# Log-sum-exp over 1024 columns: the row four from last loaded in five strided parts, 9 rows for each of eight DMA engines and 7 for each of the others

## The chip, the cores and the metric

One core of one Trainium2 chip. The metric is the device time in microseconds (us) of one execution; smaller is better. The span of a profiled execution is some 1.4 us shorter than its time.

## The reference

```python
# x: float32 (32, 512, 1024), axis = -1
x_max = np.max(x, axis=axis, keepdims=True)
return (x_max.squeeze(axis) + np.log(np.sum(np.exp(x - x_max), axis=axis))).astype(np.float32)
```

The inputs are standard normal numbers, so the kernel leaves the maximum out and computes the logarithm of the sum of exponentials.

## The kernel before

Each of the 128 partitions takes 128 rows of x that follow one another in HBM, 4 KB each. They arrive in 17 loads of falling size (4, 15, 16, 16, 16, 14, 13, 9, 7, 5, 4, 3, 2, 1, 1, 1, 1 rows a partition), all issued by SyncE into a ring of 51 rows. ScalarE (ACT) takes exponentials; VectorE (DVE) or ACT's own accumulator sums them. "Row" below is one such row of every partition: a load of 128 x 4 KB. The last four loads are one row each and all ACT's.

```python
CHUNKS = [  # rows, rows that DVE sums, parts, by halves
    # ... cut: eight loads
    (7, 7, 1, True), (5, 4, 1, True), (4, 3, 1, True), (3, 3, 1, False), (2, 2, 1, True),
    (1, 0, 1, False), (1, 0, 1, False), (1, 0, 1, False), (1, 0, 1, False),
]
# ...
    x_v = x_flat.rearrange("(p t) d -> p t d", p=P)
# ...
    def load(i):
        (s, row), r = place[i], CHUNKS[i][0]
        # ... cut: waits until the ring's rows are free
        nc.sync.dma_start(out=ring[:, s : s + r], in_=x_v[:, row : row + r]).then_inc(
            landed[i], 16
        )
# ... in the loop over loads:
        if i == len(CHUNKS) - 1:
            take_logs(logged, late_row, sums[:, logged:late_row], *done_before[-LATE])
        nc.scalar.wait_ge(landed[i], 16)
        # ... cut: exponentials for the rows that DVE sums
        for j in range(n_dve, r):
            nc.scalar.activation(out=ring[:, s + j], in_=ring[:, s + j], func=Exp,
                                 accum_out=total(row + j)).then_inc(act_done, 1)
# ... after the loop: the logarithm of the last four sums, and the store of 64 KB
```

The softmax here doesn't subtract the row's maximum and nothing guards it: scores larger than these inputs give would overflow.

## Time and profile before

| | |
|---|---|
| time, median of the first 3 runs | 162.7 us (162.52 to 162.91) |
| time, median of 6 runs, with those beside the changed kernel | 162.77 us (162.45 to 163.13) |
| span of the profiled execution | 161.5 us |
| landing of the load of three rows (12th) | 150.93 us |
| landing of the load of two rows (13th) | 153.42 us |
| landings of the last four rows | 154.70, 155.99, 157.27, 158.50 us |
| start of the last exponential | 158.56 us |

A landing is the last of the sixteen completions that the trace records for a load. The packets of the trace can be linked, each starting 3 to 9 ns before the one ahead ends, into sixteen strings, which I take for the sixteen DMA engines. Over the last six loads every string has eight packets of a load and then one of 4 bytes, its completion, load after load in the order of issue.

### The profile page before, as it was taken

Reading aid. Unit: us, or ns where it says so; the run is one execution under the profiler, and the core shown is the slowest. Engines: PE = TensorE matmul, PEld = TensorE weight load, DVE = VectorE, ACT = ScalarE, POOL = GpSimd, SP = SyncE. Lnnn points to the kernel's source line nnn. Section 1 sums busy time; section 2 is a strip of 40 time slices with the busy share of each in tenths; the row PEclk is TensorE's granted clock in tenths of the full one; section 3 lists DMA queues with packets and bytes.
Section 4 is the critical chain, followed back from the end, with each engine's and each line's share of the span. In section 5 each row is a group of like instructions: output and inputs, shape, how many; then the busy total and the mean of one; then the engine's idle time right before and its main releaser. Section 6 shows DMA issues by size and latency. Waiting matters only on the chain.

```text
span 161.5 us, 126 instructions
## 1 busy us (share of the span) xinstructions
DVE 121.0 (75%) x46; ACT 115.1 (71%) x40; POOL 0.2 (0%) x4
## 2 busy tenths in 40 slices
DVE  0028000004999999999999599999999999999892
ACT  3170006995079960999519993999199999999995
POOL 0000000000000000000000000000000000000000
DMA  7999899989799799699799999999899999999991
GB/s 268 495 487 457 350 411 520 406 373 520 308 471 520 325 455 520 276 503 520 325 422 455 455 455 438 422 422 422 366 429 438 444 433 406 441 414 423 405 407 36
DMA packets 2592, 67.18 MB, mean 416 GB/s; under 512 B 288, under 2 KB 416, under 8 KB 928
## 3 DMA queue, kind: packets, MB, share of 16 engines
q1 hardware_dynamic: 2592, 67.18, 97.3%
HBM read 67.11 MB, written 0.07 MB: 416 GB/s over the span
## 4 chain that ended last, share of the span: by engine, by line
DMA 49%; DVE 29%; ACT 20%; issue 0%
DMA ring<-in_x_dram 49%; DVE sums L157 29%; ACT ring L137 17%; ACT ring L164 3%; ACT res L108 0%
## 5 line engine op out<-in xcount | busy, mean ns | idle before, releaser
L157 DVE TENSOR_REDUCE sums<-ring 128x8 f32<-128x8192 f32 (+5 forms) x14 | 111.2, 7995 | 37.4 <-ACT ring L137 37.2
L137 ACT ACTIVATE ring<-ring 128x8192 f32<-128x8192 f32 (+6 forms) x18 | 104.4, 5836 | 44.0 <-DMA ring<-in_x_dram 43.9
L144 DVE CUSTOM_DVE_ANT_0 ring<-ring 128x512 f32<-128x512 f32 x16 | 9.9, 688 | 0.0
L164 ACT ACTIVATE ring<-ring 128x1024 f32<-128x1024 f32 x9 | 9.3, 1042 | 0.0
L122 ACT ACT_TABLE_LOAD x1 | 1.3, 1283 | 0.8 <-PEq L209 0.8
L164 ACT ACTIVATION_READ_ACCUMULATOR ring<-ring 128x1 f32 x9 | 1.6, 173 | 0.0
L144 DVE DVE_READ_ACCUMULATOR2_ANT sums<- 128x1 f32 x16 | 1.4, 85 | 0.0
L108 ACT ACTIVATE res<-sums 128x81 f32<-128x81 f32 (+1 forms) x2 | 0.5, 248 | 0.0
L108 ACT ACTIVATE res<-late 128x4 f32<-128x4 f32 x1 | 0.2, 173 | 0.0
L209 POOL MEMSET const-bfloat16-1.0<- 128x1 bf16 x1 | 0.1, 102 | 0.0
L209 POOL MEMSET const-uint8-127<- 128x1 uint8 x1 | 0.1, 102 | 0.0
L209 POOL MEMSET const-float32-0.0<- 128x1 f32 x1 | 0.1, 99 | 0.2 <-issue 0.2
L209 POOL MEMSET const-float32-1.0<- 128x1 f32 x1 | 0.1, 99 | 0.0
## 6 DMA issues: line engine op xcount, KB each, us to landing
ring<-in_x_dram SPq DMA_DIRECT2D x1, 7680.0 KB, 24.8
ring<-in_x_dram SPq DMA_DIRECT2D x1, 7168.0 KB, 29.0
ring<-in_x_dram SPq DMA_DIRECT2D x1, 6656.0 KB, 36.2
ring<-in_x_dram SPq DMA_DIRECT2D x1, 4608.0 KB, 20.3
ring<-in_x_dram SPq DMA_DIRECT2D x2, 2048.0 KB, 16.1
ring<-in_x_dram SPq DMA_DIRECT2D x1, 3584.0 KB, 28.4
ring<-in_x_dram SPq DMA_DIRECT2D x1, 2560.0 KB, 27.4
ring<-in_x_dram SPq DMA_DIRECT2D x4, 512.0 KB, 27.1
```

The source lines that it names most:

```text
L108: nc.scalar.activation(out=res[:, lo:hi], in_=src, func=Ln).then_inc(act_done, 1)
L122: nc.scalar.preload_act_table_set("natural_log_exp_and_others")
L137: nc.scalar.activation(out=ring[:, s + lo : s + hi], in_=ring[:, s + lo : s + hi], func=Exp).then_inc(act_done, 1)
L144: nc.vector.tensor_tensor_reduce(out=ring[:, s + j, : D // 2], in0=ring[:, s + j, : D // 2], in1=ring[:, s + j, D // 2 :], scale=1.0, scal ...
L157: nc.vector.reduce_sum(out=sums[:, row + lo : row + hi], in_=ring[:, s + lo : s + hi], axis=AX).then_inc(dve_done, 1)
L164: nc.scalar.activation(out=ring[:, s + j], in_=ring[:, s + j], func=Exp, accum_out=total(row + j),).then_inc(act_done, 1)
L209: nc = _bacc.Bacc("TRN2", target_bir_lowering=False, num_devices=1)
```

## The change

The sixteen completions of the last load lie 0.66 us apart (157.84 to 158.50). The intent is to give the early eight one row more and the late eight one less, once, near the end, so that the last landing comes sooner.

```diff
+UNEVEN = (13,)
+PARTS = ((0, 128, 2), (1, 128, 4), (3, 128, 8), (7, 64, 8), (71, 128, 8))
...
-        nc.sync.dma_start(out=ring[:, s : s + r], in_=x_v[:, row : row + r]).then_inc(
-            landed[i], 16
-        )
+        dst, src = ring[:, s : s + r], x_v[:, row : row + r]
+        if i not in UNEVEN:
+            nc.sync.dma_start(out=dst, in_=src).then_inc(landed[i], 16)
+            return
+        for first, last, step in PARTS:
+            nc.sync.dma_start(
+                out=dst[first:last:step], in_=src[first:last:step]
+            ).then_inc(landed[i], 16)
...
-        nc.scalar.wait_ge(landed[i], 16)
+        nc.scalar.wait_ge(landed[i], 16 * (len(PARTS) if i in UNEVEN else 1))
```

The parts have 64, 32, 16, 8 and 8 partitions: meant are 4, 2 and 1 rows for each engine, then 1 and 1 more for eight of them. "The first eight" below are the engines that take a load of eight partitions.

## The prediction

> **What bounds the kernel now.** The page of the run before gives two rows that matter at once, and I read them first:
>
> ```profile
> DVE 121.0 (75%) x46; ACT 115.1 (71%) x40; POOL 0.2 (0%) x4
> DMA  7999899989799799699799999999899999999991
> q1 hardware_dynamic: 2592, 67.18, 97.3%
> ```
>
> No compute engine is full, and the DMA row is at nine tenths or more in most slices: packets fill 97.3% of the span of 16 engines. The kernel is a stream of 67.11 MB from HBM, and compute follows it. The one question is what the end looks like: which wait ends last once the stream runs out. The changed load is one of four last loads of one row a partition (128 x 4 KB, 512 KB each), so only the last 10 us are concerned. The chain of work that ended last, from there on (start us, length us, what):
>
> ```profile
> 122.49 24.74 DMA ring<-in_x_dram
> 147.23 0.02 issue
> 147.26 2.76 ACT ring L137
> 150.02 1.04 ACT ring L164 x2
> 151.06 4.46 ACT ring L137 x2
> 155.52 3.01 ACT ring L164 x6
> 158.53 0.02 ACT res L108
> 158.55 0.01 issue
> 158.56 1.11 ACT ring L164 x2
> 159.67 0.02 issue
> 159.69 0.17 ACT res L108
> ```
>
> The last DMA on this chain landed at 147.23 us: that is the load of four rows, three loads ahead of the changed one. From there ScalarE (ACT) goes from one exponential to the next to 159.67 without a link to a DMA. So the last four loads are not named as what ended anything. How near they are to it is read from the time of issue and the time to landing of each of the four, taken alone: 129.0 + 25.7 = 154.7 us, 129.3 + 26.7 = 156.0, 129.8 + 27.5 = 157.3 and 130.3 + 28.2 = 158.5. Beside them stand the four exponentials that read them, in the timeline of ACT (start, length, engine, line):
>
> ```profile
> 155.42 1.04 ACT L164 ACTIVATE ring<-ring 128x1024 f32<-128x1024 f32 x1
> 156.42 1.05 ACT L164 ACTIVATE ring<-ring 128x1024 f32<-128x1024 f32 x1
> 157.42 1.05 ACT L164 ACTIVATE ring<-ring 128x1024 f32<-128x1024 f32 x1
> 158.42 0.24 ACT L108 ACTIVATE res<-sums 128x43 f32<-128x43 f32 x1
> 158.56 1.04 ACT L164 ACTIVATE ring<-ring 128x1024 f32<-128x1024 f32 x1
> ```
>
> Start less landing: 0.72, 0.42, 0.12 and 0.06 us. DMA delivers a row every 1.28 us, ACT uses one every 1.00 us, so ACT's lead melts by 0.28 a row and is gone at the last. An exponential that did wait for its load started 0.03 us after the landing (147.23 to 147.26), so the last one has a true slack of about 0.03 us. ACT's own order gives nearly the same start: the logarithm ahead of it began at 158.42 and the earlier logarithm of 81 columns held ACT for 0.16 us (128.31 to 128.47); this one of 43 columns, 38 fewer at 0.86 ns each (8192 columns took 7.01 us), should hold it for some 0.13, which gives 158.55 against 158.56 seen. ACT and the stream meet here within 0.03 us.
>
> [...] So parts of 64, 32 and 16 partitions give each engine 4, 2 and 1 rows, and the two parts of 8 give one more each to the first eight: 9 and 7. The trace agrees for the even load: 16 increments for each load, spread from 157.84 to 158.50 us for the last one, 0.66 us between first and last engine. It records no engine numbers, so which eight are early is not to be read.
>
> [...] Here a partition's rows lie 512 KB apart, and the steps make it 1, 2 and 4 MB. The trace shows only the 512 KB case, at 416 GB/s.
>
> **The change part by part.** No instruction of ACT, VectorE or GpSimd moves; SyncE issues five transfers in place of one.
>
> Issue: an issue of a row takes 0.33 to 0.46 us and one follows another every 0.37 to 0.48 (128.95, 129.33, 129.80, 130.28). Four more cost 4 x 0.48 = 1.9 us, so the last load is issued at 132.2 instead of 130.3. The data before it still land up to 154 us: the queue is over 20 us deep, and nothing of this reaches the path.
>
> Packets: a 4 KB packet takes 0.159 us in the best case (up to 0.172), each starting 3 ns before the one ahead ends, so 0.156 us an engine; a completion packet of 4 bytes adds about 6 ns. An engine of the first eight gets one packet and four completions more: +0.156 + 0.024 = +0.18 us. One of the others gets one packet fewer and two completions more: -0.156 + 0.012 = -0.14 us. All later loads go through the same queues in order, so these shifts stay up to the last landing.
>
> If the first eight are the early half (157.84 to 158.13), they end at 158.31 and the late half (158.14 to 158.50) at 158.36: the last landing comes 0.14 us earlier. That is the intent. But ACT gives only what its own order leaves: the last exponential can start 0.01 to 0.03 us earlier, not 0.14. Behind it come 1.11 us of exponential and its accumulator read, 0.17 of logarithm and 1.6 us of the store, all unchanged. So in the best case the change is worth 0.02 us, and about 0.1 us in executions where the stream runs a little later against ACT.
>
> In the other direction there is no cushion: a delay D of the slowest engine comes out at the end as D - 0.03 us.
>
> **The rivals.** First, the early half isn't the first eight. The completion times show a smooth spread (neighbours 0.01 to 0.12 us apart) and no gap between two halves, and the packet starts of the first load do not predict who finishes it first. Then some late engine gets +0.18 and the last landing moves to 158.68 at most: the end +0.15 us. What speaks for the intended half is only that somebody chose which half gets more.
>
> Second, the strided parts run slower than the plain row: [...]rows 4 MB apart. If that halved the rate, the packets of the row would take twice as long, 9 x 0.156 = 1.4 us more at worst; if it concerns only the three single-packet parts, 3 x 0.16 = 0.5. [...] In the profile before nothing tests it. It would make 163.1 to 164.1 us.
>
> Third, the four exponentials start to wait earlier (row three from last has 0.42 us of slack, the next 0.12). A delay above those shows as waits, but each only forwards the same D; they don't add up.
>
> **Range and chances.** Best case (-0.02 to -0.1) 0.35; a late engine loaded more (+0.15) 0.25; some slowing of the strided parts (+0.2 to +0.6) 0.3; a strong one (up to +1.4) 0.1. The middle of these is about +0.1 us on 162.7. The three runs before lie 0.39 us apart (162.52 to 162.91), which is more than the effect. I say 162.8 us, and 162.4 to 163.5. For 2% it would take 3.3 us in either direction: more than twice the worst rival, and more than the whole tail of ACT after the last landing for a gain. Faster 0.005, same 0.98, slower 0.015.
>
> **What would show it right or wrong.** In the trace after: increments of the changed load as 64 instead of 16 within the same stretch; the last landing near 158.36 (early half chosen), near 158.68 (not), or later than 158.8 (strided parts slow). The chain should still show ACT from about 147.26 on if the first holds, and a DMA as the last link before the last exponential if not. Packets of 4 KB over 0.2 us long during the changed load would show the [...]pitch rival. The prediction fails by over 0.7 us if the strided parts keep engines waiting between descriptors.

The forecast's sum came to -0.14 us at the last landing and -0.01 to -0.03 at the end in the best case, and, over all the cases, to a middle of about +0.1 us on 162.7, so 162.8. The trace after bears out the 9 and 7, and the strings of the trace before the order of the loads.

## More of the kernel before

What the stream moved near the end is in the stretches of time of the profile (stretch, length, then busy us and count of each engine, clock, DMA's busy share, GB/s):

```profile
151.00:152.00 1.00, 1.00 (x3) 1.00 (x2) 0.00 (x0) 1.00 1.04 434
153.30:154.30 1.00, 0.55 (x1) 1.00 (x2) 0.00 (x0) 1.00 1.05 418
```

The stream is full (share about 1) and moves 418 GB/s while the fourth row from last is on its way.

## The result, and the profile after

| | before | after |
|---|---|---|
| time, median of 6 runs | 162.77 us (162.45 to 163.13) | 162.69 us (162.48 to 162.92) |
| span of the profiled execution | 161.5 us | 161.2 us |
| landing of the load of three rows | 150.93 us | 150.53 us |
| landing of the load of two rows | 153.42 us | 153.03 us |
| last landing | 158.50 us | 158.22 us |

The ratio is 0.9996, with a 95% interval of 0.9979 to 1.0013. (A ratio is the mean time of one kernel's fast runs over that of the other's of the same rounds, so not quite the ratio of the medians.) The time is the same: what the change does is smaller than this interval, which is some 0.28 us to either side. The traces resolve much less than that, if one does not compare clock times. Loads that the change does not touch already land 0.4 us earlier in the trace after (150.53 for 150.93). So I count from the landing of the load of three rows, which is well ahead of the changed one, to the last landing: **7.57 us before, 7.69 after**. The last landing came 0.12 us later, not earlier.

First the page of the profile after, its count of DMA packets and the queue's share:

```profile
DMA packets 2640, 67.18 MB, mean 417 GB/s; under 512 B 336, under 2 KB 464, under 8 KB 976
q1 hardware_dynamic: 2640, 67.18, 97.4%
```

The 48 packets more than the 2592 of before are all tiny: completions, 64 in place of 16. Linked as before, each packet starting 3 to 15 ns before the one ahead ends, the trace gives eight strings with 4, 2, 1, 1 and 1 packets of the changed row and eight with 4, 2 and 1, a completion after each group: 9 and 7 as meant. (Where two packets end together the link is a choice; this one uses every packet from the load of three rows to the last.) Then the same two stretches of the trace after:

```profile
151.00:152.00 1.00, 1.00 (x5) 1.00 (x1) 0.00 (x0) 1.00 0.97 401
153.30:154.30 1.00, 0.94 (x1) 1.00 (x2) 0.00 (x0) 1.00 1.04 311
```

While the parts are moved, the engines are as busy as before (1.04) and move a quarter less: 311 GB/s for 418. The packets themselves say it: none of the 512 packets of 4 KB took over 0.19 us before (longest 0.172); after, 69 did, the longest 0.255, all of them begun between 153.28 and 154.38 us. The first 64 of 4 KB, as many as the part of step 2 has, were still at 0.16 to 0.17.

Last the tail of ACT in the timeline after:

```profile
157.03 1.05 ACT L175 ACTIVATE ring<-ring 128x1024 f32<-128x1024 f32 x1
158.03 0.24 ACT L119 ACTIVATE res<-sums 128x43 f32<-128x43 f32 x1
158.25 1.06 ACT L175 ACTIVATE ring<-ring 128x1024 f32<-128x1024 f32 x1
```

The last exponential starts 0.22 us after the logarithm, against 0.145 before (158.416 to 158.561), and 0.024 us after the last landing at 158.22. Now it waits for the load: 0.08 us. The chain of work that ended last does not name that wait:

```profile
155.12 3.02 ACT ring L175 x6
158.14 0.13 ACT res L119
158.27 0.00 ACT ring L175
158.27 0.94 issue
159.21 0.16 ACT ring L175
```

There is no DMA in it: ACT's instructions overlap (the exponential starts at 158.25 us, the logarithm ends at 158.27), so the gap that the load left probably is too small to appear as idle time; the exponential's own time is put down as "issue". A wait of under 0.1 us must be read from starts and landings.

### The profile page after: what moved, and what is told of

It reads as the page before. It is cut to its first block, busy times and chain, and to the rows that moved or that the text cites. A ratio compares the mean times of both kernels' runs of the same rounds, so it can differ in the third digit from the quotient of the medians.

```text
span 161.2 us, 130 instructions
## 1 busy us (share of the span) xinstructions
DVE 121.0 (75%) x46; ACT 115.2 (71%) x40; POOL 0.2 (0%) x4
## 4 chain that ended last, share of the span: by engine, by line
DMA 49%; DVE 29%; ACT 20%; issue 1%
DMA ring<-in_x_dram 49%; DVE sums L168 29%; ACT ring L148 17%; ACT ring L175 3%; ACT res L119 0%
```

## The experiments

All on one measure, from one trace each: from the landing of the load of three rows to the last landing ("stream"), and from the same landing to the end of the span ("tail"). D is the stream less 7.57. For the two-row load, which some expectations count from, the parts' first packets can already be in its way: in the trace after the first starts at 151.87 us, and that load lands at 153.03. Rows an engine, where an expectation names them, are as meant: counted are those of before (8) and after (9 and 7) alone.

| kernel | stream | D | tail | log to last exponential | 4 KB packets over 0.19 us | longest |
|---|---|---|---|---|---|---|
| before | 7.57 | | 10.54 | 0.145 | 0 | 0.172 |
| after | 7.69 | 0.12 | 10.64 | 0.223 | 69 | 0.255 |
| probe_before | 7.59 | 0.02 | 10.57 | 0.145 | 0 | 0.188 |
| probe_after | 7.70 | 0.13 | 10.67 | 0.230 | 62 | 0.291 |
| even_four | 7.82 | 0.25 | 10.77 | 0.221 | 71 | 0.338 |
| even_four_packed | 7.74 | 0.17 | 10.69 | 0.224 | 49 | 0.247 |
| blocks_9_7 | 8.46 | 0.89 | 11.42 | 0.229 | 172 | 0.364 |
| halves | 9.08 | 1.51 | 12.02 | 0.208 | 170 | 0.339 |
| step2_two | 7.56 | -0.01 | 10.53 | 0.145 | 0 | 0.172 |
| step8_eight | 9.22 | 1.65 | 12.18 | 0.204 | 199 | 0.472 |
| step8_packed | 8.89 | 1.32 | 11.84 | 0.224 | 175 | 0.375 |
| deal_step2 | 8.08 | 0.51 | 11.03 | 0.228 | 118 | 0.316 |
| all_four_9_7 | 9.25 | 1.68 | 12.20 | 0.444 | 211 | 0.282 |
| early_last | 6.96 | -0.61 | 10.54 | 0.145 | 0 | 0.172 |

Each line is one trace, and the traces come from several chips. Two pairs of near-equal kernels (before and probe_before, after and probe_after) lie 0.01 to 0.03 us apart, and in all 14 traces the load of three rows, which no change touches, lands 8.57 to 8.60 us after the load of five rows. So differences of 0.1 are safe to read.

A second measure from the same traces does not depend on which engine is last: the time of all 512 packets of 4 KB, shared over 16 engines, less that of before. It is 0.26 us in after and in even_four alike, 0.14 in even_four_packed, 1.20 in halves, 1.55 in step8_eight, 1.29 in step8_packed and 0.00 in step2_two. The slow packets are not all packets of the parts: halves had 170 where the changed row has 128. So rows beside it were slowed too; which packets those were was not worked out.

My theory at this point: the first eight engines are the early ones, the deal gains what was worked out, and the strided parts lose more. The rivals: the wrong half, and the uneven deal itself.

### Which engines are early: probe_before

```diff
+PROBES = (13, 15)
...
+        if i in PROBES:   # ahead of the fourth and the second row from last
+            n = PROBES.index(i)
+            nc.sync.dma_start(out=scratch[:, n], in_=x_v[0:8, n, 0:128]).then_inc(probed[n], 16)
```

> The kernel before, with two tiny loads (8 partitions, 512 bytes each) ahead of the fourth and the second load from last, each with a semaphore of its own[...]. Beside them stand the sixteen completions of the load just ahead. Theory 'intended half' (the first eight are the early ones): the eight probe completions match the eight earliest of the sixteen, within about 0.05 us. Theory 'no order': they are mixed among the sixteen, with at least two among the four latest. Last landing counted from the landing of the load ahead of the fourth from last: 5.1 us (5.08 in the profile before), within 0.1; end as before.

Which engines a load of eight partitions takes was given by a rule; what is measured is that it has eight completions.

The completions in the trace, in order of time (us):

```
two-row load   152.87 .91 .93 .96 .97 .97 153.01 .04 | 153.15 .16 .21 .26 .28 .33 .46 .53
probe          153.09 .11 .12 .15 .16 .17 .20 .22    (eight, and one of the sequencer at issue)
4th from last  154.17 .21 .24 .27 .28 .30 .31 .36    | 154.41 .43 .48 .52 .53 .61 .73 .81
```

The probe's eight come 0.18 to 0.22 us behind the eight earliest (not within the 0.05 that I expected), in nearly the same spacing; the late eight are spread over 0.38 us and the probe's over 0.14. The next load is a second witness: the eight earliest need 1.30 to 1.33 us for it, the others 1.25 to 1.28, so the earliest are those that carried the probe. The first eight are the early half here; their mean is 0.34 us ahead. "No order" falls.

### The parts without the deal: even_four

```diff
-PARTS = ((0, 128, 2), (1, 128, 4), (3, 128, 8), (7, 64, 8), (71, 128, 8))
+PARTS = ((0, 128, 2), (1, 128, 4), (3, 128, 8), (7, 128, 8))
```

> The same row in four strided parts (steps 2, 4, 8, 8) of 64, 32, 16, 16 partitions, so each engine moves 8 rows. Theory 'strided parts are slow': packets of 0.20 to 0.25 us appear again, last landing 5.25 to 5.45 us after the load ahead (before 5.08, changed kernel 5.19), spread between first and last engine still about 0.66. Rival 'the uneven deal alone is what moves the landing': packets stay at 0.16 to 0.17 us and the last landing is 5.08 to 5.15.

The last landing came 5.33 us after the two-row load; D is 0.25. The same stretch:

```profile
153.30:154.30 1.00, 1.00 (x1) 1.00 (x1) 0.00 (x0) 1.00 1.02 320
```

Slow packets without any unevenness: the parts cost 0.25 us, and the deal is not their cause. Against it, the changed kernel's 0.12 means that the deal takes 0.13 off, near the 0.14 that it was to bring. The packets took 0.26 us an engine longer in both, so the parts cost the same with and without the deal. Counted from the mean completion of the three-row load in place of its last, the deal takes 0.08 off: some 0.1 is what two traces support.

### Does the deal reach the engines: probe_after

The same two probes in the changed kernel.

> The changed kernel with the two tiny probe loads (8 partitions[...]), one ahead of the fourth row from last and one ahead of the second from last. In the kernel before with the probes the first eight were the eight earliest at both places. If the deal of 9 and 7 does what it intends: the first eight are still the earliest at the first probe, and at the second they are mixed with the others or late (0.18 + 0.14 = 0.32 us closer than before). If the deal does not reach the engines[...]: still the eight earliest at the second probe.

At the first probe the eight are again the earliest (153.08 to 153.26, 0.18 to 0.22 behind the eight earliest of the load ahead). At the second, less the same 0.2 us, they stand at 155.93 to 156.11, in the middle of the sixteen (155.82 to 156.27). The spread of the last row is 0.42 us where it was 0.58 with probes before (without probes 0.56 for 0.67). The deal does what it intends.

### Another way to 9 and 7: blocks_9_7

```diff
-PARTS = ((0, 128, 2), (1, 128, 4), (3, 128, 8), (7, 64, 8), (71, 128, 8))
+PARTS = ((0, 112, 1), (112, 120, 1), (120, 128, 1))
```

> 9 and 7 rows again, but in three unbroken blocks of 112, 8 and 8 partitions instead of strides. Theory 'strided parts are slow' with the intended half early: packets stay near 0.16 us and the last landing is about 4.95 us after the load ahead. With the wrong half: 5.2 to 5.3 with packets at 0.16. Rival 'any part of few partitions is slow, strided or not': packets of over 0.2 us, landing over 5.15.

5.72 us after the two-row load, D = 0.89. My theory in its form "strides are slow" falls: without a stride it is worse. Something else of the parts is slow. The slow packets began at 152.19 us, 0.40 us after the first packet of the row, when, by an estimate from 0.156 us a packet, no engine can have been past its third packet. The large part comes first, with seven rows an engine if dealt evenly. So the part of 112 partitions is among the slow ones, not only the two of 8.

### The whole at four times the size: all_four_9_7

```diff
-UNEVEN = (13,)
+UNEVEN = (13, 14, 15, 16)
```

> All four last rows dealt 9 and 7 in five strided parts. Theory 'strided parts cost some 0.29 us an engine and row' (mean shift of the sixteen completions in the changed kernel): 4 x 0.29 = 1.2, and the first eight 4 x 0.18 - 0.33 = 0.4 later than the late half was: last landing some 1.5 us later, time 164.1 to 164.5. Rival 'the parts cost nothing but the deal': +0.4 us, 163.1; wrong half: +0.7, 163.4.

164.17 us (163.93 to 164.46, 5 runs) against 162.37 for before on the same chip: ratio 1.0113 (1.0098 to 1.0128). D = 1.68, and the time rose by 1.80, the same within the noise. Here clock times show the cost most plainly (deal_step2, below, shows a smaller one), and it goes with the parts being slow; the deal alone would have made +0.4 or +0.7.

### HBM or the SBUF side: even_four_packed, halves

even_four_packed has the parts of even_four and this:

```diff
-                out=dst[first:last:step], in_=src[first:last:step]
+                out=dst[first:last:step], in_=x_flat[first * P : first * P + len(range(first, last, step))]
```

> Four strided parts, 8 rows an engine, as in the run with the even deal, but each part reads rows that lie one after another in HBM (a pitch of 4 KB in place of 1, 2 and 4 MB); the SBUF side is the same. The result is wrong on purpose. Theory 'the pitch in HBM makes the parts slow': packets back to 0.16 to 0.17 us and the last landing 5.05 to 5.15 us after the load ahead. Theory 'the SBUF side[...]': packets of over 0.2 us again, last landing 5.25 to 5.45.

"SBUF side" means here only what is left when the addresses in HBM are not the cause.

5.24 us, just under the range of the SBUF side and outside that of the pitch; 49 slow packets for 71. By itself undecided. (The record calls the runs with wrong results, this one, step8_packed and early_last, correct: its check does not notice such errors.)

```diff
-PARTS = ((0, 128, 2), (1, 128, 4), (3, 128, 8), (7, 64, 8), (71, 128, 8))
+PARTS = ((0, 64, 1), (64, 128, 1))
```

> The row in two unbroken halves, partitions 0 to 63 and 64 to 127: no stride, 8 rows an engine, 512 KB pitch in HBM as in the kernel before. Theory 'pitch in HBM' and theory 'strides': no slow packets, last landing 5.05 to 5.15 us after the load ahead. Theory 'SBUF side': [...]packets of up to 0.31 us and the last landing up to 8 x 0.156 = 1.25 us later, about 6.0 to 6.3; at least 5.5.

6.07 us after the two-row load, D = 1.51. The stretch again:

```profile
153.30:154.30 1.00, 0.86 (x1) 0.75 (x2) 0.00 (x0) 1.00 1.10 250
```

No stride and the pitch of before, and the rate fell from 418 to 250 GB/s with busy engines. The HBM pitch cannot be the cause here. Nor is it the number of parts: step2_two, below, has two parts as well and loses nothing.

### Which part: step2_two, step8_eight, step8_packed

```diff
-PARTS = ((0, 128, 2), (1, 128, 4), (3, 128, 8), (7, 64, 8), (71, 128, 8))
+PARTS = ((0, 128, 2), (1, 128, 2))                   # step2_two
+PARTS = tuple((k, 128, 8) for k in range(8))         # step8_eight and step8_packed
```

step8_packed also reads rows that lie one after another, as even_four_packed does.

> The row in two parts of step 2 (even and odd partitions, 64 each, 4 rows an engine each): 8 rows an engine. In the changed kernel the packets were still 0.16 us while most engines were in the part of step 2, and over 0.2 only after it. Theory 'the parts of step 8, one row an engine, are the slow ones': few or no packets over 0.19 us, last landing 7.57 to 7.65 us after the landing of the load of three rows (7.57 and 7.60 before, 7.82 with the four even parts). Rival 'any part of fewer than 128 partitions is slow, as the two halves were': 7.8 or later.

> The row in eight parts of step 8 (16 partitions, one row an engine each): 8 rows an engine. Theory 'the parts of step 8 are the slow ones': packets of 0.2 to 0.3 us over the whole row, last landing at 8.1 or later (8 packets, each at least 0.06 slower, +0.5 on 7.6). Rival 'only the change from one dealing to another is slow': 7.85 or less.

> The same eight parts of step 8, each read from rows that lie one after another in HBM (wrong on purpose), so the 4 MB pitch is gone and the SBUF side stays. Theory 'HBM pitch': last landing 7.6 to 7.75. Theory 'SBUF side': within 0.15 of the run with the pitch. Both together: in between.

One line of each, in this order: the first two parts cost nothing, the eight cut the rate to about a half.

```profile
153.30:154.30 1.00, 0.88 (x1) 1.00 (x2) 0.00 (x0) 1.00 1.01 406
```

```profile
153.30:154.30 1.00, 0.69 (x1) 0.39 (x2) 0.00 (x0) 1.00 1.01 225
```

```profile
153.30:154.30 1.00, 1.00 (x1) 0.71 (x1) 0.00 (x0) 1.00 1.09 250
```

D is -0.01, 1.65 and 1.32. Parts of 64 partitions with step 2 are free; those of 16 with step 8 are slow. Packing the rows takes off 0.33 of 1.65, which is what was expected for "both together", and 0.08 of 0.25 in the four parts (of the packets' time 0.26 of 1.55 and 0.12 of 0.26). So the pitch may have a share, from one look each: a small one in the eight parts, a third to a half in the four. With the source packed, most of the loss in the eight parts remains, which leaves the SBUF side or the way the rows are dealt.

### A deal of step 2 alone: deal_step2

```diff
-PARTS = ((0, 128, 2), (1, 128, 4), (3, 128, 8), (7, 64, 8), (71, 128, 8))
+PARTS = ((0, 128, 2), (1, 97, 2), (97, 113, 2), (113, 128, 2))
```

> 9 and 7 rows again, with step 2 alone: parts of 64, 48, 8 and 8 partitions (4, 3, 1 and 1 rows). Theory 'step 8 is the slow part, the deal itself is right': last landing 7.43 to 7.55, earlier than before; the last exponential starts 0.145 us after the logarithm (ACT bound) and the time is still that of before within noise. Rival 'the short parts are slow whatever their step': 7.65 or later and the last exponential waits for it.

D = 0.51, 163.05 us (162.88 to 163.44, 4 runs) against 162.54: ratio 1.0025 (1.0009 to 1.0042). Theory "step 8 alone is slow" falls too: a small step does not save this deal. The run does not tell the part of 48 partitions from the two of 8.

### What an earlier landing is worth: early_last

```diff
+        w = D // 2 if i == len(CHUNKS) - 1 else D
-        nc.sync.dma_start(out=ring[:, s : s + r], in_=x_v[:, row : row + r]).then_inc(
+        nc.sync.dma_start(out=ring[:, s : s + r, :w], in_=x_v[:, row : row + r, :w]).then_inc(
...
+                scale=1e-3 if i == len(CHUNKS) - 1 else 1.0,
```

> The kernel before with the last load cut to 512 of 1024 columns, so that it lands some 0.6 us earlier; the last exponential still covers 1024 columns (half of them stale, scaled by 0.001 so that nothing overflows; the result is wrong on purpose). Theory 'ACT's own order leaves only 0.01 to 0.03 us': the last exponential starts 0.12 to 0.14 us after the start of the logarithm ahead of it, not 0.145, and the time is that of before within noise, 0 to 0.1 us faster. Rival 'the last landing sets the end': 0.5 to 0.6 us faster.

The last landing came at 157.34 us, 0.61 earlier on the measure of the table. The tail of ACT:

```profile
157.86 0.24 ACT L109 ACTIVATE res<-sums 128x43 f32<-128x43 f32 x1
158.00 1.04 ACT L165 ACTIVATE ring<-ring 128x1024 f32<-128x1024 f32 x1
```

The last exponential starts 0.145 us after the logarithm (157.859 to 158.004), to the nanosecond what it did before and not the 0.12 to 0.14 that I expected, and the tail is 10.54, as before. The time is 162.34 against 162.56 with a ratio of 0.9997 (0.9980 to 1.0015). So in this trace nothing is to be had from an earlier last landing; the times alone would not resolve a gain of 0.1 us.

## Why the prediction was right, and where it was not

The time, 162.69 us for 162.8 predicted, is inside 162.4 to 163.5 and the same as before. That alone says little, since the noise is wider than the effect. By its steps:

- **The meeting of ACT and the stream within 0.03 us: right, and the delay passes through as D - 0.03.** The table tests it over a wide range: 10.54 + D - 0.03 gives 10.63 for after (measured 10.64), 10.76 for even_four (10.77), 11.40 for blocks_9_7 (11.42), 12.02 for halves (12.02) and 12.16 for step8_eight (12.18).
- **The best case of 0.01 to 0.03 us: too large.** I worked out that the logarithm of 43 columns would hold ACT for 0.13 us. early_last shows 0.145 with the data there for 0.6 us. ACT's order was the whole bound and the gain of an earlier landing was zero in that trace. The gain of about 0.1 us that I gave to executions with a later stream was not tested.
- **The deal of -0.14 us: right within what can be read**, 0.13 (0.08 on the other count) by even_four against after. That the first eight are the early half was left at better than even; the probe shows it, in these executions.
- **The strided parts: the rival happened, at a smaller size than its figures.** I gave 0.5 us if the three parts of single rows were slow; the row cost 0.25. Of the reasons given with it one, rows 4 MB apart, is no cause in halves (512 KB, D = 1.51) and a small one in step8_eight (0.33 of 1.65), but in even_four, the nearest to the change, packing took off a third of D (0.08 of 0.25). The argument against a strong slowing did not hold for parts that are slow throughout: in step8_eight the packets took 1.55 us an engine longer, where a doubling of 8 packets of 0.156 would be 1.25.
- **The sum failed in its mixture, not in its middle.** I weighed a best case against slow parts as alternatives. Both came at once: -0.13 from the deal and +0.25 from the parts make +0.12, of which 0.03 fell into ACT's slack, so some +0.09 at the end. The middle of my weights was +0.1; that the two agree is luck, since no entry of my list had both.
- **Issue: off, without effect.** I took 4 x 0.48 = 1.9 us. A strided part took 0.57 to 0.66 us to issue for 0.33 of the plain row, and the next row's issue came 3.22 us after the first part, not 0.37: 2.85 us more. The data in front still filled the queue until 153 us.
- **The signs to look for: partly badly chosen.** I gave clock times (158.36, 158.68, 158.8) for the last landing. 158.22 would have read as the gain, when the whole stream was 0.4 us ahead in that execution. Only the distance from an untouched load tells. Nor does the chain name the DMA in the changed kernel, as I had said it would. The engines were not kept waiting either: from the load of three rows on, each packet of the trace after starts 3 to 15 ns before the one ahead ends, and it is the packets that are longer (up to 0.255 us).

On the mechanism: it is not shown. step2_two and halves both have two parts of 64 partitions, and one loses nothing (-0.01 us) while the other loses 1.51. So what sets them apart is which partitions a part holds, not its size or the number of parts, and it is not the pitch in HBM, since halves has that of before. Eight parts of 16 with step 8 lose 1.65 (1.32 packed), and four parts of which two are such lose 0.25 (0.17 packed). Why these are slow no run here tells, and the traces give no rule for other splits. Not separated either: what of deal_step2 is due to its part of 48 and what to its parts of 8.

No version here beats both kernels. step2_two is as fast as before, and in the trace of early_last an earlier last landing gained nothing while ACT's own order filled the tail; a real gain would have to shorten ACT's work too.

## What to carry to other kernels

Before moving load from late DMA engines to early ones, ask who takes over when the load comes sooner: here another engine was due within 0.03 us, so a gain of 0.14 could pay nothing and a loss would pay in full. If a load is split by partitions, test the split in a trace first: two parts of even and odd partitions cost nothing here, while two unbroken halves (1.51 us) and parts of every eighth partition (1.65 us) cost more than the row of 1.28 us itself. Measure effects of a tenth of a microsecond inside one trace, from a landing that the change cannot touch, not between clock times of two executions.
